# A ConvFFN's up projection as seven sub-products in PSUM, and its down projection in a phase of its own

## The chip, the cores and the metric

The kernel runs on one core of a Trainium2 chip. The metric is device microseconds from start to end of one launch; lower is better. The engines are called as in the profile: PE (matmul), PEld (its weight loads), DVE, ACT, POOL and SP; SP's queue issues all DMAs here.

## The reference, cut to what matters

One layer: a token mixer (a Fourier branch and a gated DeltaNet branch), then a ConvFFN. The change lies in the ConvFFN and in the stage just ahead of it. T = 1024 tokens, D = 1024 channels, D_FF = 2816, all fp32; the tokens form a grid of 16 by 64.

```python
def ffn_sublayer(stream, shift, scale, gate, g_pre, g_post, w_up, conv_w, w_down, rows, cols):
    h = modulate(rms_norm(stream, g_pre), shift, scale)
    a, u = jnp.split(h @ w_up, 2, axis=-1)
    a = dwconv2d(a, conv_w, rows, cols)
    y = (jax.nn.silu(a) * u) @ w_down
    return stream + gate * rms_norm(y, g_post)
```

Here `a` is the gate, which goes through a 3x3 depthwise convolution, and `u` the value. `stream` is the mixer's output, `x + gt1 * rms_norm(merged @ w_out)`.

## The kernel before, in words

**Precision.** Every fp32 factor is split into a high part (rounded to fp32r, a copy) and a low part (the rest, a subtraction). A product of two factors is three matmuls: high by high, high by low, low by high. `halves` loads a weight and splits it (ACT copies the high part, DVE or POOL subtracts), `product` runs the three matmuls per 128 rows of the contraction, `split` splits an activation.

**Order.** The code does not issue instructions where it calls them. It records them (`Program.record`), finds their dependencies through tiles, buffers and banks, and gives each a planned cost; `Program.schedule` then issues them, engine by engine, along their longest paths to the end. Every engine works through its own instructions in that order. All instructions therefore have line 349 in the profile, and tiles are named by number: `p` is a PSUM bank, `m` an SBUF buffer, `d` a buffer in DRAM.

**Ahead of the ConvFFN** (from L1460). For each of eight tiles of 128 tokens, `w_out` is multiplied with the merged branches (48 matmuls of 128x512 into two banks), `post` squares the result on ACT, takes the root on POOL, scales it and adds the residual on DVE. The tile is stored to `x1d`, normed again, and after four tiles (one half of the tokens, g = 0 or 1) transposed on PE: eight transposed blocks per half, which ACT modulates (`hh`), DVE casts to a high part and POOL subtracts to a low part: `h2H[k][g]`, `h2L[k][g]` (L1484 to L1488).

**The ConvFFN** goes over 22 chunks of 128 hidden channels. `up_a(c)` (L1507) multiplies the gate's 1024x128 weights with both halves of the tokens, 24 matmuls of 128x512 for each; ACT copies the result into a padded grid `apad`; DVE runs the nine taps of the convolution over 128x1024 in SBUF (`acc`, one TENSOR_SCALAR and eight SCALAR_TENSOR_TENSOR, L1515 to L1520), ACT takes tanh for the silu, DVE finishes it. `up_u(c)` (L1527) does the value's 48 matmuls, multiplies with `acc` on DVE and splits the gated product into `gH`, `gL`.

After every group of two or three chunks (`groups`, L1538) `down` multiplies these with their rows of `w_down`: for each of the eight token tiles 6 matmuls per chunk into two banks, and DVE adds the banks to `y2[t]`, an fp32 sum in SBUF. In the last group each token tile is squared, scaled by its root and by the gate row, added to `x1d`'s rows, which are loaded into one of two buffers, and stored.

So the up projection has 22 x 2 x 2 x 24 = 2112 matmuls of 128x512 and the down projection 22 x 8 x 6 = 1056. PSUM has eight banks: X0, X1, Y0, Y1, pd, pm, pp, pf; up alternates between pp and pf, down takes the six others.

Of the kernel before, what the change touches and what calls it, by code (L numbers as in the profile page):

```python
# [16 lines left out]
P = 128  # L17
# [470 lines left out]
def layer(prog, a, out):  # L488
# [23 lines left out]
    # ---------------------------------------------------------------- constants  # L512
# [12 lines left out]
    # ---------------------------------------------------------------- weights  # L525
# [33 lines left out]
    # ---------------------------------------------------------------- hidden states  # L559
# [12 lines left out]
    # ---------------------------------------------------------------- modulation, pre-norm  # L572
# [93 lines left out]
    # ---------------------------------------------------------------- decay and beta  # L666
# [75 lines left out]
    # ---------------------------------------------------------------- conv of q, k, v  # L742
# [30 lines left out]
    # ---------------------------------------------------------------- delta rule: preparation  # L773
# [86 lines left out]
    def merge_blocks(name, LTs, bk, k2):  # L860
# [11 lines left out]
        # 32 -> 64  # L872
# [30 lines left out]
        # 64 -> 128  # L903
# [19 lines left out]
    # ---------------------------------------------------------------- context pass  # L923
# [128 lines left out]
    # ---------------------------------------------------------------- latent pass  # L1052
# [185 lines left out]
    # ---------------------------------------------------------------- Fourier branch  # L1238
# [68 lines left out]
    # ---------------------------------------------------------------- branch gates, gated delta output  # L1307
    mp = pool("mH", bufs=17, side="right")
# [90 lines left out]
    mf = [[m_tile(mp, f"mf{k}{g}", F32) for g in range(2)] for k in range(KT)]  # L1399
# [13 lines left out]
    # ---------------------------------------------------------------- merge of the branches  # L1413
    lp = pool("mL", bufs=17, side="right")
# [4 lines left out]
    for k in range(KT):  # L1419
        wl = weights(a["wf"][k], f"wf{k}")  # L1420

        def usef(g, hs, pt):
            t_ = gt.tile([P, HALF], F32, tag="t", name=f"tf{k}{g}")
            gl = gt.tile([P, HALF], F32, tag="gl", name=f"g0l{k}{g}")
            sp.dma_start(gl, gd[0, k, :, hs])
            ve.scalar_tensor_tensor(t_, gl, 1.0, pt, op0=ALU.add, op1=ALU.mult)
            ve.tensor_tensor(t_, t_, mf[k][g], op=ALU.add)
            mH[k][g] = h_ = m_tile(mp, f"mH{k}{g}")
            mL[k][g] = l_ = m_tile(lp, f"mL{k}{g}")
            se.activation(h_, t_, AF.Copy, scale=0.5)  # L1430
            ve.scalar_tensor_tensor(l_, t_, 0.5, h_.bitcast(F32), op0=ALU.mult, op1=ALU.subtract)
# [16 lines left out]
    def post(y2, res, grow_, name, pl, tags=("jk", "pt"), nb=2):  # L1448
        sq = const.tile([P, 2], F32, tag="sq", name=f"sq_{name}", bufs=4)
        for g in range(2):  # L1450
            se.activation(pl.tile([P, HALF], F32, tag=tags[0], name=f"jk_{name}{g}", bufs=nb), y2[g], AF.Square,
                          scale=D ** -0.5, accum_out=sq[:, g:g + 1])
        mean_pow(sq)
        for g in range(2):
            hs = slice(g * HALF, (g + 1) * HALF)
            t_ = pl.tile([P, HALF], F32, tag=tags[1], name=f"pt_{name}{g}", bufs=nb)
            ve.scalar_tensor_tensor(t_, y2[g], sq[:, 1:2], grow_[:, hs], op0=ALU.mult, op1=ALU.mult)
            ve.tensor_tensor(res[:, hs], res[:, hs], t_, op=ALU.add)

    xn = []  # L1460
    for t in range(8):
        xt = wp.tile([P, D], F32, tag="xt", name=f"xr{t}", bufs=6)
        sp.dma_start(xt, a["x"][t * P:(t + 1) * P, :])
        pts = [ps(f"{'XY'[g]}{t % 2}", [P, HALF], f"wo{t}{g}") for g in range(2)]
        n = 0
        for k in range(KT):
            ts_ = slice((t % 4) * P, (t % 4 + 1) * P)
            for m_, w_ in ((mH[k][t // 4], wo[k][0]), (mH[k][t // 4], wo[k][1]), (mL[k][t // 4], wo[k][0])):
                for g in range(2):
                    te.matmul(pts[g], m_[:, ts_], w_[:, g * HALF:(g + 1) * HALF], start=n == 0, stop=n == 23)  # L1470
                n += 1
        post(pts, xt, g1r, f"o{t}", wp)
        sp.dma_start(x1d[t * P:(t + 1) * P, :], xt)
        ss = rms(xt, f"n2_{t}", wp.tile([P, D], F32, tag="junk", name=f"junk2_{t}", bufs=1))
        ve.tensor_scalar(xt, xt, ss, None, op0=ALU.mult)
        xn.append(xt)
        if t % 4 == 3:
            g = t // 4

            def dst(k):  # L1480
                h2H[k][g] = m_tile(mp, f"h2H{k}{g}")
                h2L[k][g] = m_tile(lp, f"h2L{k}{g}")
                return h2H[k][g], h2L[k][g]
            for k in range(KT):  # L1484
                pt = transposed(xn[-4:], k, f"h2{g}", ("pd", "pm")[k % 2])
                hh = wp.tile([P, HALF], F32, tag="hh", name=f"hh{k}{g}")
                se.activation(hh, pt, AF.Identity, scale=mod2[:, 8 + k:9 + k], bias=mod2[:, k:k + 1])
                split(*dst(k), hh, ve, po)  # L1488
# [3 lines left out]
    # ---------------------------------------------------------------- ConvFFN  # L1492
    yp = pool("y2", bufs=1)
    y2 = [yp.tile([P, D], F32, name=f"y2_{t}") for t in range(8)]
    dwp = pool("wd", bufs=3)
    fpl = pool("ffn", bufs=2, side="right")
    cf = fpl.tile([P, NC_FF, 9], F32, name="cf", bufs=1)
# [6 lines left out]
    def h2(g):
        return lambda k: (h2H[k][g], h2L[k][g])

    def up_a(c):  # L1507
        wl = weights(a["wu"][c], f"ua{c}")
        ap_ = apad[c % 2]

        def use(g, hs, pt):
            se.activation(ap_[:, 1 + 8 * g:9 + 8 * g, 1:GW + 1], pt.rearrange("p (a b) -> p a b", b=GW), AF.Copy)
        proj_rows(wl, h2, f"ua{c}", use)
        acc = fpl.tile([P, GR, GW], F32, tag="acc", name=f"acc{c}")
        ve.tensor_scalar(acc, ap_[:, 1:GR + 1, 1:GW + 1], cf[:, c, 4:5], None, op0=ALU.mult)  # L1515
        for i in range(9):
            if i != 4:
                dy, dx = i // 3, i % 3
                ve.scalar_tensor_tensor(acc, ap_[:, dy:dy + GR, dx:dx + GW], cf[:, c, i:i + 1], acc,
                                        op0=ALU.mult, op1=ALU.add)  # L1520
        acc = acc.rearrange("p a b -> p (a b)")
        th_ = fpl.tile([P, T], F32, tag="th", name=f"th{c}", bufs=1)
        se.activation(th_, acc, AF.Tanh)
# [128 lines left out]
```

## Time and profile before

| what | us |
|---|---|
| runs, median of 3 (lowest to highest) | 2151.86 (2146.21 to 2153.07) |
| profiled execution, span from first to last instruction | 2152.6 |
| first ConvFFN weight load issued (trace) | 1263.2 |
| last token tile of `w_out` squared by ACT (trace) | 1373.0 |
| first store of the output issued (trace) | 2114.2 |

The profile comes from one execution of its own, of which the page gives the span alone. Views used below: the page (busy time by engine, and in 40 slices), windows (busy time of each engine in stretches), groups (instructions of one engine, operation and shape: count, busy time, mean ns of one, idle time ahead of them and what ended it), the chain of work that ended last, and the timeline (start, length, engine, operation, count, and in brackets the idle time ahead and its releaser).

### The profile page before, as it was taken

To read this page: it belongs to the slowest core of one execution; us is meant where nothing else is said; L and a number is where in the kernel's file an instruction comes from. 1 tells how busy PE (TensorE), PEld (TensorE's weight loads), DVE (VectorE), ACT (ScalarE), POOL (GpSimd) and SP (SyncE) were. 2 spreads that over 40 slices of the span, in tenths; PEclk is the share of its full clock that TensorE was granted. 3 is DMA by queue.
4 is the path that set the end of the run, shared out by engine and by line. 5 is a ranking of instruction groups with operands and counts; after the bars stand their busy time and mean duration, and the time that the engine had idled before them with its cause. 6 is when DMAs were issued, how large, how long until landed. Compare 5 with 4: busy or idle time off the path is not lost. (4 is left out here: it accounts for less than half of the span.)

```text
span 2152.6 us, 31012 instructions
## 1 busy us (share of the span) xinstructions
PE 2023.2 (94%) x11734; PEld 1623.3 (75%) x11734; DVE 1378.7 (64%) x2608; ACT 740.5 (34%) x1740; POOL 486.8 (23%) x479
## 2 busy tenths in 40 slices
PE   6989999898979989999999999989999999999996
PEld 2777878786768777788777778768888888888885
DVE  7548767676677566653656492587465757475655
ACT  6365454453244433533421142422231222112212
POOL 4131121324233442441311000412010110101005
PEclk9999999899999999999999999989999999999998
DMA  7152323462342444332778561311111111111114
GB/s 274 47 190 83 105 84 126 130 195 66 97 134 84 120 128 114 101 105 76 230 251 292 165 220 42 105 40 44 40 59 35 54 49 45 50 45 50 49 49 147
DMA packets 164216, 232.32 MB, mean 108 GB/s; under 512 B 74097, under 2 KB 87250, under 8 KB 164066
## 3 DMA queue, kind: packets, MB, share of 16 engines
q1 hardware_dynamic: 164066, 230.34, 33.3%
q8 instruction: 92, 1.51, 0.3%
q14 instruction: 58, 0.48, 0.1%
HBM read 180.89 MB, written 49.40 MB: 107 GB/s over the span
## 5 line engine op out<-in xcount | busy, mean ns | idle before, releaser
L349 PE MATMUL p<-m,m 128*128 128x512 f32 (+5 forms) x11574 | 2009.4, 340 | 106.2 <-DVE m L349 65.5
L349 PEld LDWEIGHTS p<-m,m 128*128 128x128 f32 (+3 forms) x11574 | 1604.4, 174 | 501.6 <-ACT m L349 68.8
L349 POOL TENSOR_TENSOR m<-m,m 128x512 fp32r<-128x512 f32 (+6 forms) x244 | 380.5, 1572 | 1332.0 <-ACT m L349 532.6
L349 ACT ACTIVATE m<-m 128x512 fp32r<-128x512 f32 (+6 forms) x563 | 390.3, 711 | 775.0 <-DMA m<-in_wu_dram 254.4
L349 DVE TENSOR_TENSOR m<-m,m 128x512 fp32r<-128x512 f32 (+23 forms) x940 | 483.3, 521 | 192.7 <-ACT m L349 166.4
L349 DVE SCALAR_TENSOR_TENSOR m<-m,m,m 128x1024 f32<-128x1024 f32 (+2 forms) x260 | 304.2, 1176 | 37.8 <-DMA m<-in_w_ada_dram 24.4
L349 ACT ACTIVATE m<-p 128x128 f32<-128x128 f32 (+5 forms) x444 | 181.7, 427 | 336.9 <-PE p L349 309.2
L349 DVE SCALAR_TENSOR_TENSOR m<-p,m,m 128x128 f32<-128x128 f32 (+4 forms) x472 | 191.0, 442 | 110.3 <-ACT m L349 57.6
L349 ACT ACTIVATE m<-p,m 128x128 f32<-128x128 f32 (+2 forms) x240 | 115.6, 492 | 235.8 <-PE p L349 219.8
L349 DVE TENSOR_TENSOR m<-m,p 128x512 f32<-128x512 f32 (+3 forms) x229 | 123.8, 569 | 105.9 <-PE p L349 105.8
L349 DVE SCALAR_TENSOR_TENSOR m<-m,m 128x512 f32<-128x512 f32 (+6 forms) x141 | 107.0, 768 | 36.6 <-ACT m L349 29.1
L349 DVE COPY m<-p 32x256 f32<-32x256 f32 (+10 forms) x116 | 42.0, 367 | 64.0 <-ACT m L349 38.5
L349 POOL COPY m<-m 32x256 f32<-32x256 f32 (+2 forms) x136 | 53.6, 397 | 115.3 <-DMA m<-d 73.5
L349 DVE SCALAR_TENSOR_TENSOR m<-m,m,p 128x128 f32<-128x128 f32 x128 | 42.8, 342 | 41.5 <-PE p L349 40.2
L349 DVE TENSOR_SCALAR m<-m,m 128x1024 f32<-128x1024 f32 x44 | 35.2, 799 | 49.1 <-ACT m L349 36.0
L349 POOL MEMSET m<- 128x1024 f32 (+7 forms) x79 | 35.1, 456 | 134.9 <-PE p L349 101.6
L349 ACT ACTIVATE p<-p 128x128 f32<-128x128 f32 x208 | 55.3, 266 | 20.6 <-PE p L349 18.6
L349 DVE STREAM_TRANSPOSE m<-m 32x256 f32<-32x256 f32 (+1 forms) x50 | 24.5, 491 | 29.1 <-DMA m<-d 28.4
L349 DVE CAST m<-m 128x512 fp32r<-128x512 f32 (+3 forms) x45 | 26.3, 593 | 25.0 <-ACT m L349 23.4
L349 ACT ACTIVATION_READ_ACCUMULATOR p<-p 128x1 f32 x208 | 40.0, 192 | 0.0
L349 DVE TENSOR_TENSOR m<-p,m 128x512 f32<-128x512 f32 (+4 forms) x47 | 28.1, 608 | 11.9 <-PE p L349 11.7
L349 POOL TENSOR_SCALAR_AFFINE_SELECT m<-m 128x1024 f32<-128x1024 f32 x16 | 19.0, 1207 | 72.2 <-DVE m L349 72.2
(20 smaller groups left out, 130.4 us busy)
## 6 DMA issues: line engine op xcount, KB each, us to landing
m<-d SPq DMA_DIRECT2D x76, 512.0 KB
m<-d SPq DMA_DIRECT2D x114, 256.0 KB
m<-in_wi_dram SPq DMA_DIRECT2D x106, 256.0 KB
m<-in_w_ada_dram SPq DMA_DIRECT2D x48, 512.0 KB
d<-m SPq DMA_DIRECT2D x94, 256.0 KB
m<-in_wu_dram SPq DMA_DIRECT2D x88, 256.0 KB
m<-in_wn_dram SPq DMA_DIRECT2D x22, 512.0 KB
m<-in_x_dram SPq DMA_DIRECT2D x16, 512.0 KB
```

Source lines behind the costliest of these rows:

```text
L349: return getattr(engine.real, method)(*[real(v) for v in args], **{k_: real(v) for k_, v in kw.items()})
```

## The change

**The up projection becomes a 2x2 block product.** For each chunk the weights are four 128x512 blocks: gate and value (`a`, `u`), by the lower and upper half of the contraction (`a0`, `a1`, `u0`, `u1`). The hidden state is four blocks too: halves of the contraction by halves of the tokens. Instead of eight block products there are seven, of sums of blocks (Strassen's):

- M2 = (u0+u1) H00, M5 = (a0+a1) H11, M1 = (a0+u1)(H00+H11), M4 = u1 (H10-H00), M3 = a0 (H01-H11), M7 = (a1-u1)(H10+H11), M6 = (u0-a0)(H00+H01).
- Bank A gets M2, then M4 and M7 on top; bank B gets M5, then M3 and M6; bank C gets M1. Between these steps the bank is read: A after M2 by ACT (into `v_`, negated), after M4 by ACT (the value of the first tokens), after M7 by DVE; B after M5 by DVE, after M3 by ACT (the gate of the second tokens), after M6 by DVE. `v_` = M1 - M2 - M5.

Each M is 12 matmuls of 128x512 (`chain`), 84 for a chunk, 1848 in all. The sums of weight blocks (five for a chunk) and all seven low parts of a chunk are formed on POOL, the high parts copied by ACT (`summed`, `split_w`). The sums of the hidden state's blocks are formed once, ahead of the chunks, 16 of them and 28 splits in seven rings of four (`sum_b`, `side_b`), by DVE, POOL and ACT.

**The convolution** runs in two halves of 128x512 whose running sum `acc` lies in a PSUM bank (pd, pm); ACT forms its first tap. The gated product is not split at once but stored to DRAM (`gdr`).

**The down projection is a phase of its own**, after all chunks, in blocks of three, three and two token tiles. Each block keeps its banks over all 22 chunks, so there is no sum in SBUF: 1056 matmuls as before. It loads its part of `gdr`, splits it on ACT and POOL, and keeps 20 of the 22 chunks' split `w_down` rows in SBUF. In the last three chunks of a block the tiles follow one another, and each is normed, added and stored as soon as its bank is complete.

**Ahead of it**, the last two token tiles of `w_out` run side by side (the other six one after another as before), the second norm uses the same helper as the first (`root`), and pools and bank names change.

```diff
-    mp = pool("mH", bufs=17, side="right")
+    mp = [pool(f"mH{g}", bufs=9, side="right") for g in range(2)]
...
-    lp = pool("mL", bufs=17, side="right")
+    lp = [pool(f"mL{g}", bufs=8, side="right") for g in range(2)]
...
+    rings = {1: (mp[0], mp[0]), 3: (lp[0], lp[0]), 4: (mp[1], mp[1]), 2: (lp[1], lp[1])}
+    RB = {}
+    def side_b(m, src, n):
+        hp, lp_ = rings[m]
+        h_, l_ = m_tile(hp, f"bH{m}{n}"), m_tile(lp_, f"bL{m}{n}")
+        (ve.tensor_copy(h_, src) if n % 2 else se.activation(h_, src, AF.Copy))
+        (ve, po)[n % 2].tensor_tensor(l_, src, h_.bitcast(F32), op=ALU.subtract)
+        RB.setdefault(m, []).append((h_, l_))
+    def sum_b(m, x_, y_, op, n):
+        t_ = hb.tile([P, HALF], F32, tag="hs", name=f"hs{m}{n}", bufs=2)
+        (ve, po)[(m + n) % 2].tensor_tensor(t_, x_, y_, op=op)
+        side_b(m, t_, n)
...
-    for t in range(8):
+    for ts in ((0,), (1,), (2,), (3,), (4,), (5,), (6, 7)):
...
+        for k in (0, 4, 1, 5, 2, 6, 3, 7) if g == 0 else (4, 5, 6, 7, 0, 1, 2, 3):
+            pt = transposed(xn[-4:], k, f"h2{g}", ("pd", "pm")[k % 2])
+            hh[k, g] = hb.tile([P, HALF], F32, tag=f"hh{g}", name=f"hh{k}{g}")
+            se.activation(hh[k, g], pt, AF.Identity, scale=mod2[:, 8 + k:9 + k], bias=mod2[:, k:k + 1])
+            if g == 0 and k < 4:
+                side_b(1, hh[k, 0], k)
+            elif g == 0:
+                sum_b(3, hh[k, 0], hh[k - 4, 0], ALU.subtract, k - 4)
+            elif k >= 4:
+                side_b(4, hh[k, 1], k - 4)
+    for i in range(4):
+        sum_b(2, hh[i, 1], hh[i + 4, 1], ALU.subtract, i)
...
+    def chain(pt, w_, m, start):
+        n = 0
+        for i in range(4):
+            ks = slice(i * P, (i + 1) * P)
+            h_, l_ = RB[m][i]
+            for x_, r_ in ((w_[0], h_), (w_[0], l_), (w_[1], h_)):
+                te.matmul(pt, x_[:, ks], r_, start=start and n == 0, stop=n == 11,
+                          skip_group_check=not start)
+                n += 1
+    def split_w(src, name, fresh=None):
+        h_ = wq.tile([P, HALF], F32R, tag="h", name=f"qh_{name}", bufs=WH)
+        se.activation(h_, src, AF.Copy)
+        l_ = wq.tile([P, HALF], F32R, tag="l", name=f"ql_{name}", bufs=WL) if fresh else wq.over(src, F32R, f"ql_{name}")
+        po.tensor_tensor(l_, src, h_.bitcast(F32), op=ALU.subtract)
+        return h_, l_
+    def both(c):
...
+        chain(A, summed("u0", "u1", ALU.add, "m2"), 1, True)
+        se.activation(v_, A, AF.Copy, scale=-1.0)
+        chain(B, summed("a0", "a1", ALU.add, "m5"), 4, True)
+        ve.tensor_tensor(v_, v_, B, op=ALU.subtract)
+        chain(C, summed("a0", "u1", ALU.add, "m1"), 0, True)
+        ve.tensor_tensor(v_, v_, C, op=ALU.add)
+        chain(A, split_w(raw["u1"], f"m4{c}", True), 3, False)
+        se.activation(u_[:, 0:HALF], A, AF.Copy)
+        chain(B, split_w(raw["a0"], f"m3{c}", True), 2, False)
+        se.activation(inner(1), grid(B), AF.Copy)
+        chain(A, summed("a1", "u1", ALU.subtract, "m7"), 6, False)
+        ve.tensor_tensor(inner(0), grid(A), grid(v_), op=ALU.add)
+        chain(B, summed("u0", "a0", ALU.subtract, "m6"), 5, False)
+        ve.tensor_tensor(u_[:, HALF:T], B, v_, op=ALU.add)
+        for g in range(2):
+            hs = slice(g * HALF, (g + 1) * HALF)
+            acc = ps(("pd", "pm")[g], [P, GR // 2, GW], f"acc{c}{g}")
+            se.activation(acc, inner(g), AF.Copy, scale=cf[:, c, 4:5])
...
+            ve.tensor_tensor(th_, th_, u_[:, hs], op=ALU.mult)
+            sp.dma_start(gdr[c, :, hs], th_)
...
+    for blk, ts in enumerate(((0, 1, 2), (3, 4, 5), (6, 7))):
...
+        for n, c in enumerate(first[:-tail]):
+            gs[c] = down_g(c)
+            for t in ts:
+                down_mm(t, c, n)
...
+        for t in ts:
+            for n, c in enumerate(first[-tail:]):
+                down_mm(t, c, NC_FF - tail + n)
+            xt = fin.tile([P, D], F32, tag="xt", name=f"xo{t}")
+            sp.dma_start(xt, x1d[t * P:(t + 1) * P, :])
+            r = root(pts[t], f"f{t}", fin)
```

How the order of the instructions moves shows best where the hidden state's second half is ready and the first chunk begins. **POOL, before:** the end of the hidden state's splits. The eight rows with a size of 128x512 are low parts (a modulated block minus its high part); the last one is the first low part of a gated product, some chunks later.

```order
L349 TENSOR_TENSOR m_10430<-m_10965,m_10416 128x512
L349 TENSOR_TENSOR m_10474<-m_10970,m_10463 128x512
L349 TENSOR_TENSOR m_10479<-m_10965,m_10469 128x512
L349 TENSOR_TENSOR m_10546<-m_10970,m_10530 128x512
L349 TENSOR_TENSOR m_10538<-m_10965,m_10526 128x512
L349 TENSOR_TENSOR m_10598<-m_10970,m_10587 128x512
L349 TENSOR_TENSOR m_10590<-m_10965,m_10580 128x512
L349 TENSOR_TENSOR m_10646<-m_10970,m_10636 128x512
L349 TENSOR_TENSOR m_11460<-m_11349,m_11454 128x512 x2
```

**POOL, now,** the same place, up to the first operation for chunk 1's weights: m_10992 and m_10965 are sums of two blocks of the hidden state (`hs`), the rows that read m_10992 make its low part (those of m_10965 are made on DVE); m_11234 is the low part of u0 - a0 of chunk 0, m_11176 the sum u0 + u1 of chunk 1.

```order
L350 TENSOR_TENSOR m_10992<-m_10928,m_11256 128x512
L350 TENSOR_TENSOR m_11234<-m_11165,m_11209 128x512
L350 TENSOR_TENSOR m_11351<-m_10992,m_11343 128x512
L350 TENSOR_TENSOR m_10992<-m_10989,m_11270 128x512
L350 TENSOR_TENSOR m_11369<-m_10992,m_11365 128x512
L350 TENSOR_TENSOR m_10992<-m_10961,m_11256 128x512
L350 TENSOR_TENSOR m_10965<-m_10923,m_11292 128x512
L350 TENSOR_TENSOR m_11380<-m_10992,m_11378 128x512
L350 TENSOR_TENSOR m_10992<-m_11198,m_11270 128x512
L350 TENSOR_TENSOR m_10965<-m_10984,m_11308 128x512
L350 TENSOR_TENSOR m_11390<-m_10992,m_11388 128x512
L350 TENSOR_TENSOR m_11176<-m_11128,m_11126 128x512
```

Where POOL had eight low parts and then nothing for long, it now has, between the second half's first low part and m_11176 (both counted), 19 operations of this size, two of them for chunk 0's weights and one, the last, for chunk 1's.

**PE, now,** at the same place (pieces in order; p_124 is bank C with M1 of chunk 0, p_192 bank A of chunk 1 with M2, p_197 bank A of chunk 0 with M4):

```order
L350 MATMUL p_124<-m_11365,m_11215 128x512
L350 MATMUL p_124<-m_11369,m_11215 128x512
L350 MATMUL p_124<-m_11365,m_11241 128x512
L350 MATMUL p_192<-m_10933,m_11215 128x512
L350 MATMUL p_192<-m_10271,m_11215 128x512
L350 MATMUL p_197<-m_10286,m_11114 128x512
L350 MATMUL p_197<-m_10339,m_11114 128x512
L350 MATMUL p_197<-m_10286,m_11187 128x512
```

Two products of chunk 1, which need the copy of m_11176, stand ahead of M4 of chunk 0; M2, M5 and M1 of chunk 0, 36 products, stand ahead of them and behind the last product of `w_out`. Before, 142 products of the up projection stood between the last product of `w_out` and the first product of chunk 2's gate.

More of the change, by code (lines that the diff above doesn't have):

```diff
@@ L1489, in layer @@
     close(wp)
     close(wop)
[L1493 to L1497, printed above, removed]
+    wq = pool("wq", bufs=5, side="right")
+    wq.sizes = {"r": HALF}
+    RAW, WH, WL = 8, 5, 5
+    h2p = pool("h2p", bufs=24, side="right")
+    for m in (0, 6, 5):
+        rings[m] = (h2p, h2p)
+    for i in range(4):
+        sum_b(2, hh[i, 1], hh[i + 4, 1], ALU.subtract, i)
@@ L1498, in layer @@
+    for i in range(4):
+        sum_b(0, hh[i, 0], hh[i + 4, 1], ALU.add, i)
+    for i in range(4):
+        sum_b(6, hh[i + 4, 0], hh[i + 4, 1], ALU.add, i)
+    for i in range(4):
+        sum_b(5, hh[i, 0], hh[i, 1], ALU.add, i)
+    close(hb)
+    upr = pool("upr", bufs=1, side="right")
+    gst = pool("gst", bufs=4)
+    upl = pool("upl", bufs=1)
+    cf = upl.tile([P, NC_FF, 9], F32, name="cf")
     sp.dma_start(cf, a["cf"])
     ve.tensor_scalar(cf, cf, 0.5, None, op0=ALU.mult)
-    apad = [fpl.tile([P, GR + 2, GW + 2], F32, name=f"apad{i}", bufs=1) for i in range(2)]
+    apad = [upl.tile([P, GR + 2, GW + 2], F32, name=f"apad{i}") for i in range(2)]
@@ L1501, in layer @@
     for t_ in apad:
         po.memset(t_, 0.0)
[L1504 to L1508, printed above, removed]
-        ap_ = apad[c % 2]
[L1511 to L1523, printed above, removed]
-        ve.scalar_tensor_tensor(acc, th_, 1.0, acc, op0=ALU.add, op1=ALU.mult)
-        return acc
@@ L1527, in up_u @@
-    def up_u(c, acc):
-        wl = weights(a["wu"][NC_FF + c], f"uu{c}")
-        gH = fpl.tile([P, T], F32R, tag="gH", name=f"gH{c}", bufs=4)
-        gL = fpl.tile([P, T], F32R, tag="gL", name=f"gL{c}", bufs=4)
-        def use(g, hs, pt):
-            ve.tensor_tensor(acc[:, hs], acc[:, hs], pt, op=ALU.mult)
-            split(gH[:, hs], gL[:, hs], acc[:, hs], se, po)
-        proj_rows(wl, h2, f"uu{c}", use)
-        return gH, gL
-    groups = [3, 3, 3, 3, 3, 2, 2, 3]
-    g2r = yp.tile([P, D], F32, name="g2r")
@@ L1540, in layer @@
[L1540 to L1556 removed]
+    gdr = dram.tile([NC_FF, P, T], F32, name="gdr")
@@ new lines, in layer, with down_w @@
+    for c in range(NC_FF):
+        both(c)
+    for p_ in (upr, h2p, wq, lp[1], lp[0], mp[1], mp[0], upl):
+        close(p_)
+    wn = pool("wn", bufs=1, side="right")
+    fin = pool("fin", bufs=2)
+    g2r = fin.tile([P, D], F32, name="g2r", bufs=1)
+    sp.dma_start(g2r, grow[1:2, :].broadcast_to([P, D]))
+    held = {}
+    def down_w(c, at):
+        if held.get(at, (None,))[0] != c:
+            h_ = wn.tile([P, D], F32R, tag=f"h{at}", name=f"dh{c}_{at}")
+            w_ = wn.tile([P, D], F32, tag=f"l{at}", name=f"dw{c}_{at}")
+            sp.dma_start(w_, a["wn"][c * P:(c + 1) * P, :])
+            held[at] = (c, (h_, split_over(wn, h_, w_, f"dl{c}_{at}")))
+        return held[at][1]
@@ L1566, in down @@
[L1566 to L1584 removed]
+                t_ = fin.tile([P, HALF], F32, tag="pt", name=f"pf{t}{g}")
```

171 lines of the change are left out of this document (98 added, 73 removed).

## The prediction

> **What bounds the kernel now.** I read the page first, then windows over the ConvFFN, then the chain of waits, then the groups and the timeline at the two ends of the ConvFFN.
>
> ```profile
> PE 2023.2 (94%) x11734; PEld 1623.3 (75%) x11734; DVE 1378.7 (64%) x2608; ACT 740.5 (34%) x1740; POOL 486.8 (23%) x479
> ...
> 1600.00:1800.00 200.00, 200.00 (x861) 160.87 (x860) 125.51 (x132) 40.30 (x59) 18.75 (x13) 1.00 0.14 47
> 1800.00:2000.00 200.00, 200.00 (x864) 161.44 (x863) 127.32 (x133) 42.26 (x62) 20.00 (x13) 1.00 0.15 48
> ...
> 1655.63 100.66 PE p L349 x432
> 1756.30 100.43 PE p L349 x432
> ```
>
> The page says PE, 94%. The windows (length; then busy time and instructions of PE, PEld, DVE, ACT, POOL; granted clock, DMA share, GB/s) say it for the ConvFFN alone: PE is busy for all of 200 us at full clock, POOL for a tenth, DMA for 15%. The chain of waits has nothing but PE there: 432 products, which is three chunks of up and down, in 100.43 us, **0.2325 us a product** (864 in 200 us gives the same). In this stage a product less is 0.2325 us less, as long as no other engine becomes later than PE.
>
> At the two ends of the ConvFFN PE does wait:
>
> ```profile
> 1373.02 0.60 ACT L349 ACTIVATE m<-p 128x512 f32<-128x512 f32 x1 [3.33 <-PE p L349]
> 1375.33 1.40 DVE L349 SCALAR_TENSOR_TENSOR m<-p,m,m 128x512 f32<-128x512 f32 x2
> 1375.49 1.29 POOL L349 TENSOR_TENSOR m<-m,m 128x512 fp32r<-128x512 f32 x1 [0.39 <-DVE m L349]
> 1376.65 1.29 DVE L349 TENSOR_TENSOR m<-m,m 128x512 f32<-128x512 f32 x2
> 1386.00 1.28 POOL L349 TENSOR_TENSOR m<-m,m 128x512 fp32r<-128x512 f32 x1 [5.03 <-DVE m L349]
> 1389.30 1.28 POOL L349 TENSOR_TENSOR m<-m,m 128x512 fp32r<-128x512 f32 x1 [0.36 <-DVE m L349]
> 1389.78 1.08 DVE L349 CAST m<-m 128x512 fp32r<-128x512 f32 x1 [0.56 <-ACT m L349]
> 1390.94 1.27 POOL L349 TENSOR_TENSOR m<-m,m 128x512 fp32r<-128x512 f32 x1 [0.36 <-DVE m L349]
> 1427.14 3.32 PE L349 MATMUL p<-m,m 128*128 128x512 f32 x7 [4.94 <-DVE m L349]
> ...
> 2079.67 52.51 PE L349 MATMUL p<-m,m 128*128 128x512 f32 x227
> 2147.62 1.42 DVE L349 SCALAR_TENSOR_TENSOR m<-m,m,m 128x512 f32<-128x512 f32 x2 [1.22 <-DMA m<-d]
> ```
>
> At the **hand-over** from `w_out` to the ConvFFN, ACT squares the last token tile at 1373.02, so its products have just ended. 13.0 us later (1386.00) POOL makes the first low part of the hidden state's second half. Up to 1427.14, 54.1 us, PE runs the 142 products that stand there in its order, worth 33.0 us: **21.1 us are lost**. At the **end** the last product is over at 2079.67 + 52.51 = 2132.2 and the span ends at 2152.6: a tail of **20.4 us**, in which output tiles are loaded, added and stored through two buffers.
>
> **The change, part by part.** The sum is made against the profiled span, 2152.6, which is 0.7 above the median of the runs.
>
> *Products removed.* A chunk's up projection falls from 96 products to 84, over 22 chunks 264 products: 264 x 0.2325 = **61.4 us less**, if PE stays the bound. The down projection's 1056 products keep their number, shape and order of banks; I take the same rate. PE's time for a chunk is 84 x 0.2325 = 19.5 us, and each other engine must fit into that.
>
> ```profile
> L349 DVE SCALAR_TENSOR_TENSOR m<-m,m,m 128x1024 f32<-128x1024 f32 x96 | 123.2, 1284 | 2.4
> ...
> L349 DVE TENSOR_TENSOR m<-m,p 128x512 f32<-128x512 f32 x156 | 100.3, 684 | 75.2 <-PE p L349 75.1
> L349 DVE TENSOR_TENSOR m<-m,m 128x512 f32<-128x512 f32 x48 | 32.1, 697 | 9.8 <-DMA m<-d 9.8
> L349 DVE SCALAR_TENSOR_TENSOR m<-m,m,m 128x512 f32<-128x512 f32 x32 | 31.4, 1011 | 9.1 <-DMA m<-d 5.8 <-POOL m L349 3.0
> L349 DVE SCALAR_TENSOR_TENSOR m<-m,p 128x512 f32<-128x512 f32 x32 | 21.3, 683 | 11.0 <-PE p L349 6.6 <-DMA m<-d 4.1
> L349 DVE SCALAR_TENSOR_TENSOR m<-p,m,m 128x512 f32<-128x512 f32 x16 | 11.3, 746 | 4.0 <-POOL m L349 4.0
> ...
> L349 ACT ACTIVATE m<-m 128x512 fp32r<-128x512 f32 x294 | 181.9, 629 | 544.2 <-DMA m<-in_wu_dram 254.4 <-PE p L349 117.5 <-DVE m L349 81.6
> L349 ACT ACTIVATE m<-p,m 128x512 f32<-128x512 f32 x80 | 56.8, 721 | 124.9 <-PE p L349 110.6 <-POOL m L349 9.7 <-DVE m L349 4.5
> L349 ACT ACTIVATE p<-m 128x512 f32<-128x512 f32 x16 | 9.4, 588 | 24.6 <-DVE m L349 24.6
> ...
> 1501.25 3.91 POOL L349 TENSOR_TENSOR m<-m,m 128x512 fp32r<-128x512 f32 x2 [20.30 <-ACT m L349]
> ```
>
> *POOL* gets 12 operations a chunk (five sums, seven low parts) where it had two. Alone one takes 1.28 (1386.00). Beside DVE work it takes longer: 3.91 for two at 1501.25. The rows at 1389 show how: a DVE cast begins while POOL works, ends only 0.36 after POOL's operation, and then POOL goes on, so two such operations exclude each other. At 1375.33 two DVE operations that read one tensor from PSUM and one from SBUF run beside POOL's, and neither is longer than alone (1.40 for two, 1.29). The new DVE work of a chunk is nearly all of that kind: the convolution's sum, four evictions and two silu steps each have their second tensor in PSUM. Only two multiplications by `u_` read two tensors from SBUF, 0.70 each. So 12 x 1.28 + 2 x 0.70 = 16.8 us, under 19.5. The bounds are 15.4 (nothing in the way) and 12 x 1.96 = 23.5 (all as at 1501.25); I take 16.8, as the rows at 1375 are the nearer.
>
> *DVE* writes into PSUM, which no row of before shows. Its 16 taps of 128x512: the nearest rows are the 746 ns of an operation that reads PSUM and a scalar, and two of these in 1.40, that is 0.66 from start to start; in the order the two halves' taps mostly alternate, so that one seldom waits for the one just ahead. ACT's rows show no price for a PSUM target (588 against 629). From below 16 x 0.66 = 10.6, from above 16 x 1.01 = 16.2 (the group with three SBUF operands); I take 0.70, 11.2. Four evictions at 0.684, two silu steps at 0.683 and two multiplications at 0.697 make 5.5 more. 16.7 us, under 19.5; the ends are 16.1 and 21.7.
>
> [...]
>
> *ACT*: seven copies (0.63), three evictions and two first taps (0.72 at most), two tanh (0.63): 9.3 us, hidden. *DMA*: four 256 KB loads as before and two 256 KB stores, 1.5 MB in 19.5 us, about 80 GB/s; in the down phase 0.7 MB in 18 x 0.2325 = 4.2 us, 170 GB/s. The window below moved 236 GB/s while PE worked for 99% of it, so I cost the way through DRAM at nothing. Were that cover gone, each 10% of the down phase would cost 1056 x 0.2325 x 0.1 = 25 us.
>
> ```profile
> 1000.00:1200.00 200.00, 198.24 (x873) 153.37 (x872) 118.52 (x169) 56.43 (x110) 39.26 (x29) 1.00 0.71 236
> ```
>
> *Sums in SBUF removed.* 112 DVE additions (684 ns) and 16 ACT copies of the old down projection go. They lay beside PE, which never waited there: nothing gained. *Up to down:* the split rows of `w_down` lie over the rings of the hidden state, and the first ring ends with M2 of the last chunk, six sub-products (72 products, 16.7 us) before the end; load, copy and subtraction fit. What is late next is the first tile in banks X1 and Y1, which must wait until DVE has evicted the last chunk: 0.25 + 0.68 + 0.25, with the same at block ends, **1.5 us**, bounds 0 and 8.
>
> *The hand-over* gets worse. Count from T, the square of the last token tile. T + 13.0 as before until the first low part. Then POOL has 19 operations up to the sum for chunk 1's weights: 24.3 us at 1.28. Beside them DVE has 15 sums and low parts with two SBUF inputs (0.70) and eight casts (0.36), 13.4 us, and these and POOL's exclude each other. So that sum is ready between T + 37.3 and T + 50.7; both queues are dense, so I take T + 48, near the upper end. ACT copies it (0.63) and PE goes on at T + 48.7. The products of chunk 0 that follow (M4, M3, M7, M6) and everything after are queued behind the waiting one, though M4's operands have long been there; ahead of it PE had 36 products, 8.4 us. Lost: 40.3 instead of 21.1, **19.2 us more**, bounds 8.5 and 22. The slow products after such a wait (7 in 3.32 us at 1427.14) come in both. After it POOL, at 16.8 us a chunk, gains on PE.
>
> *The tail* gets shorter. All token tiles but the last are stored under PE, and the last one's rows of `x1d` are already loaded. The steps are those at 1373.02: from the square to the end of the second addition (1376.65 + 1.29) 4.9 us, 0.25 ahead of it, and from the last DVE operation (2147.62 + 1.42 = 2149.0) to the end of the span 3.6: 8.8 us instead of 20.4, **11.6 us less**, bounds 8 and 12.
>
> Sum: 2152.6 - 61.4 + 1.5 + 19.2 - 11.6 = 2100.3, against the median 0.7 less: **2100 us**, 2.4% faster.
>
> **The rivals.**
>
> 1. *The cheap hand-over* (0.15): DVE's work there falls into POOL's gaps. T + 37.3 holds, 10.7 us less: 2089. For it: POOL waited 0.36 between operations at 1389, so there are gaps; against it: that wait was DVE's own use of the lock.
> 2. *PE waits in each chunk* (0.22): its order runs three sub-products side by side, and bank B's next sub-product needs DVE's subtraction from `v_`, behind taps already begun. One tap (0.70) and a release (0.3) late in each chunk is 22 x 1.0: 2122. For it: DVE would be busy for 86% of a chunk. Against it: M1 and M4 stand between, up to 24 products, 5.6 us.
> 3. *DVE paces the up phase* (0.06): above (19.5 - 5.5)/16 = 0.875 us a tap DVE is later than PE. At 0.95 it is 20.7 us a chunk, 1.2 x 22 = 26 more: 2126.
> 4. *POOL paces it, and the kernel is slower* (0.07): this begins where a POOL operation takes 19.5/12 = 1.63 on average. It eats all the gain (51.6 us, 2.35 a chunk) at 1.82. At the 1.96 of 1501.25 a chunk takes 23.5, 4.0 x 22 = 88 more: 2188. For it: before shows just this price wherever POOL worked in the ConvFFN beside taps. Against it: those taps had three operands in SBUF, the new ones have their sum in PSUM.
>
> That products don't go is no rival: the order has 264 fewer.
>
> **How the numbers follow.** My forecast has 0.47, for 2095 to 2110; the rivals 0.15, 0.22, 0.06 and 0.07; 0.03 is left for a total between, within 0.3% of before, which is about what a measurement of this kernel can tell from no change. The range goes from 2084 (cheap hand-over with an up-to-down step of nothing and the tail's best) to 2128 (rivals 2 and 3); it leaves out rival 4 and the rest, and some of each edge. Faster by over 0.3%: 0.90, within 0.3%: 0.03, slower: 0.07.
>
> **What would show it.** In the changed profile, 84 products a chunk at 0.23 us without idle time; POOL near 1.3 us an operation in the up phase and 80 to 90% busy, DVE near 85%; a PE wait of 10 us or more on ACT or POOL before chunk 1's first product; about 9 us from the last product to the end. The prediction fails if chunks take over 20.5 us, if POOL's mean is over 1.6, or if the down phase waits for DMA.

## The result, and the profile after

The changed kernel takes **2098.5 us** (median of 4 runs, 2097.32 to 2099.22) against 2151.24 of the kernel before beside it (4 runs): the ratio is 0.9754, 95% interval 0.9742 to 0.9765, 2.5% faster. The forecast was 2100. Its profiled span is 2096.8 us, 55.8 less than before's.

First the page of after (busy time, share of the span and instructions of each engine), then two windows, one in the up phase and one in the down phase (start and end; length; busy time and instructions of PE, PEld, DVE, ACT, POOL; granted clock, DMA share, GB/s):

```profile
PE 1960.3 (93%) x11470; PEld 1580.9 (75%) x11470; DVE 1355.2 (65%) x2714; ACT 827.6 (39%) x1934; POOL 822.5 (39%) x757
...
1450.00:1830.00 380.00, 379.29 (x1674) 313.64 (x1673) 333.17 (x469) 168.94 (x285) 319.72 (x243) 1.00 0.26 90
1850.00:2070.00 220.00, 220.00 (x937) 176.47 (x936) 57.99 (x72) 47.43 (x96) 63.50 (x64) 1.00 0.32 103
```

264 products are gone (11734 - 11470), and PE is the bound of both phases: it waits 0.7 us in the 380 of the first window and not at all in the second. But a product takes 380/1674 = 0.227 us in the up phase and 220/937 = 0.235 us in the down phase, where the prediction had 0.2325 for both. POOL is busy for 84%, DVE for 88%.

The groups of DVE and POOL between 1500 and 1800 us (busy time, mean ns of one; idle time before them):

```profile
L350 DVE SCALAR_TENSOR_TENSOR p<-m,m,p 128x512 f32<-128x512 f32 x252 | 171.4, 749 | 2.2
L350 DVE TENSOR_TENSOR m<-m,m 128x512 f32<-128x512 f32 x32 | 40.9, 1301 | 0.5
...
L350 POOL TENSOR_TENSOR m<-m,m 128x512 fp32r<-128x512 f32 x110 | 149.1, 1365 | 29.0 <-PE p L350 23.8 <-ACT m L350 5.1
L350 POOL TENSOR_TENSOR m<-m,m 128x512 f32<-128x512 f32 x80 | 106.3, 1329 | 19.4 <-PE p L350 19.3 <-POOL m L350 0.2
```

The taps, whose sum is in PSUM, take 749 ns, and POOL's operations 1.33 to 1.37 us beside them. The multiplications by `u_`, with two tensors from SBUF, take 1.30 us where 0.70 was priced; they are the only DVE operations here with both tensors in SBUF.

The hand-over, from the timeline (start, length, engine, operation; idle time before it and who ended it):

```profile
1372.41 0.58 ACT L350 ACTIVATE m<-p 128x512 f32<-128x512 f32 x1
...
1419.02 2.76 POOL L350 TENSOR_TENSOR m<-m,m 128x512 fp32r<-128x512 f32 x2 [0.36 <-DVE m L350]
1421.82 0.63 ACT L350 ACTIVATE m<-m 128x512 fp32r<-128x512 f32 x1 [2.50 <-POOL m L350]
1422.50 1.22 PE L350 MATMUL p<-m,m 128*128 128x512 f32 x2 [9.81 <-ACT m L350]
1424.30 1.73 DVE L350 TENSOR_TENSOR m<-m,m 128x512 f32<-128x512 f32 x1 [1.20 <-POOL m L350]
1426.12 0.60 ACT L350 ACTIVATE m<-p 128x512 f32<-128x512 f32 x1 [3.68 <-DVE m L350]
1426.77 5.57 PE L350 MATMUL p<-m,m 128*128 128x512 f32 x14 [3.05 <-ACT m L350]
```

T, the square of the last token tile, is at 1372.41. PE goes on at 1422.50 = T + 50.1, as ACT has copied the sum of chunk 1's weights (forecast T + 48.7). Two products later it stops **again**: ACT's next eviction (1426.12, bank A of chunk 0 into `v_`) has waited 3.68 us for a DVE sum that ends at 1426.03 (1424.30 + 1.73). PE has nothing to do with that sum. The prediction had no such wait.

The end (last products; last DVE step):

```profile
2079.71 9.32 PE L350 MATMUL p<-m,m 128*128 128x512 f32 x39
...
2092.33 1.28 DVE L350 TENSOR_TENSOR m<-m,m 128x512 f32<-128x512 f32 x2
```

The last product is over at 2089.03, the span at 2096.8: a tail of 7.8 us instead of 20.4.

### The profile page after: what moved, and what is told of

Read it like the earlier page. It is cut to its first block, busy times and chain, and to the rows that moved or that the text cites. A ratio compares the mean times of both kernels' runs of the same rounds, so it can differ in the third digit from the quotient of the medians.

```text
span 2096.8 us, 31434 instructions
## 1 busy us (share of the span) xinstructions
PE 1960.3 (93%) x11470; PEld 1580.9 (75%) x11470; DVE 1355.2 (65%) x2714; ACT 827.6 (39%) x1934; POOL 822.5 (39%) x757
## 5 line engine op out<-in xcount | busy, mean ns | idle before, releaser
L350 PE MATMUL p<-m,m 128*128 128x512 f32 (+6 forms) x11310 | 1946.5, 339 | 125.9 <-DVE m L350 66.6
L350 PEld LDWEIGHTS p<-m,m 128*128 128x128 f32 (+4 forms) x11310 | 1562.0, 174 | 500.6 <-ACT m L350 78.1
L350 POOL TENSOR_TENSOR m<-m,m 128x512 fp32r<-128x512 f32 (+8 forms) x522 | 716.8, 1393 | 946.9 <-ACT m L350 424.2
L350 ACT ACTIVATE m<-m 128x512 fp32r<-128x512 f32 (+8 forms) x655 | 428.0, 668 | 651.9 <-DMA m<-d 165.7
L350 DVE TENSOR_TENSOR m<-m,m 128x512 f32<-128x512 f32 (+23 forms) x940 | 512.0, 552 | 74.5 <-ACT m L350 53.0
L350 ACT ACTIVATE m<-p 128x512 f32<-128x512 f32 (+4 forms) x510 | 220.0, 447 | 329.9 <-PE p L350 290.4
L350 DVE SCALAR_TENSOR_TENSOR p<-m,m,p 128x512 f32<-128x512 f32 x352 | 240.1, 748 | 3.0
L350 DVE SCALAR_TENSOR_TENSOR m<-m,m 128x512 f32<-128x512 f32 (+5 forms) x119 | 76.4, 649 | 27.7 <-ACT m L350 19.6
L350 DVE TENSOR_TENSOR m<-m,p 128x128 f32<-128x128 f32 (+3 forms) x117 | 53.4, 458 | 33.2 <-PE p L350 32.4
L350 DVE SCALAR_TENSOR_TENSOR m<-m,m,m 128x1024 f32<-128x1024 f32 (+2 forms) x68 | 59.6, 877 | 23.6 <-DMA m<-in_w_ada_dram 23.2
```

The source lines that it names most:

```text
L350: return getattr(engine.real, method)(*[real(v) for v in args], **{k_: real(v) for k_, v in kw.items()})
```

## The experiments

Medians are of each kernel's own runs. A ratio is to the kernel before on the same chip, with its 95% interval; for the changed kernel it is 0.9754.

### Moving addresses only

What differs between the two phases is not the instruction. The stationary tiles of the down products, `gh` and `gl`, lie on the left stack of SBUF behind the constants, whose size (1603 words) is odd; those of the up products lie on the right stack, at whole multiples of 64 bytes (all such places are counted by the pools' sizes, from the start of the kernel's SBUF area in a partition). Three kernels differ from the changed one in unused words alone; all instructions keep their order on every engine.

```
     held = {}
+    const.tile([P, 13], F32, name="pad")     # 1 and 5 words in the other two
```

> The changed kernel with 13 words of unused space behind the constants: same instructions, same order, but every tile of the left stack starts 52 bytes further on (the stationary tiles gh and gl of the down products at a multiple of 64 bytes in a partition, and not 12 bytes behind one). Theory 'placement' (a product whose stationary tile starts off such a boundary goes slower): the down products go from one every 0.2353 us to one every 0.2267 us, as the up products do, so 1056 x 0.0086 = -9.1 us there, a few us more from the mixer's products whose tiles stand 12 bytes off, together 2084 to 2090 us against 2098.5. Rival 'stage' (the rate belongs to the pattern of the down products, two products of one stationary tile into two banks): step stays 0.235, time 2097 to 2100.

> The same with 1 word of unused space: the left stack starts at 16 bytes behind a multiple of 64, on a multiple of 16 but not of 32. Theory 'placement' with a 16-byte boundary: as with 13 words, down products at 0.2267 us, 2084 to 2090 us. 'Placement' with a boundary of 32 or 64 bytes: little or nothing gained, down products still above 0.230 us, 2094 to 2100. Rival 'stage': 0.235, 2097 to 2100.

> The changed kernel with 5 unused words behind the constants: the stationary tiles of the down products start 32 bytes behind a multiple of 64 (12 behind one in the changed kernel: 0.2353 us a product; 16 behind: 0.2319; at one: 0.2268). If the boundary that counts is 32 bytes, 0.2268 us and 2086 to 2090; if it is 64 bytes, about 0.229 to 0.234 us and 2090 to 2098.

The down window of the three (13 words, 1 word, 5 words):

```profile
1850.00:2070.00 220.00, 220.00 (x972) 182.10 (x971) 56.26 (x70) 47.32 (x97) 64.63 (x67) 1.00 0.33 104
```

```profile
1850.00:2070.00 220.00, 220.00 (x951) 178.02 (x950) 55.36 (x69) 45.54 (x94) 63.93 (x66) 1.00 0.32 101
```

```profile
1850.00:2070.00 220.00, 220.00 (x944) 176.72 (x943) 57.84 (x72) 47.23 (x96) 63.49 (x64) 1.00 0.33 104
```

| unused words | offset of `gh`, `gl` mod 64 bytes | products in 220 us | time | ratio |
|---|---|---|---|---|
| 0 | 12 | 937 | 2098.5 | 0.9754 |
| 1 | 16 | 951 | 2097.43 | 0.9740 (0.9724 to 0.9755) |
| 5 | 32 | 944 | 2097.19 | 0.9755 (0.9724 to 0.9787) |
| 13 | 0 | 972 | 2087.12 | 0.9696 (0.9682 to 0.9711) |

PE has no idle time in any of these windows, at full clock. Of the four places only the multiple of 64 bytes makes the down products as fast as the up products; 16 and 32 are not enough. 1056 products gain 8.9 us by it (1056 x (0.2348 - 0.2263)), the kernel 11.4 (its profiled span 9.5). The rest was not followed up; T alone, ahead of all this, moves by up to 3.45 us between these four kernels, from 1368.96 with 1 word to 1372.41 with none. "Stage" is refuted for these products.

The same for the kernel before, and then with the moving tile of its down products at a wider boundary (432 more words behind the tiles `y2`, ahead of the pool `dwp`):

```
+    const.tile([P, 13], F32, name="pad")
     ...
+    fpl.tile([P, 2], F32, name="pad2")
     cf = fpl.tile([P, NC_FF, 9], F32, name="cf", bufs=1)
```

> The kernel before with the same 13 words, and 2 words more ahead of cf on the right stack, so that the stationary and the moving tiles of the up products and of the down products all start at a multiple of 64 bytes. 'Placement': up products from 0.2336 to about 0.227 us (2112 x 0.0066 = -14), down products from 0.230 to 0.227 (1056 x 0.0035 = -3.7), a few us more in the mixer: 2130 to 2136 us, and of the change's gain some 8 us was placement. Rival 'stage': 2149 to 2153.

> The kernel before as in the run with 13 words, with 432 more unused words, so that the moving tile of its down products starts at a multiple of 2048 bytes instead of 320 bytes behind one, as all moving tiles do that went at 0.2267 us. Theory 'the moving tile needs a wider boundary': its down products go from 0.2305 to 0.227 us, 1056 x 0.0035 = -3.7 us, 2136 to 2140 us. Rival 'interleaving' (the down products of this kernel are slower since they alternate with up products or share banks with the sums): 0.2305 stays, 2141 to 2144.

One window over the ConvFFN, of before, of before with 13 + 2 words, and with 432 more:

```profile
1450.00:2070.00 620.00, 620.00 (x2669) 499.47 (x2668) 396.26 (x408) 137.85 (x204) 62.45 (x38) 1.00 0.14 47
```

```profile
1450.00:2070.00 620.00, 619.92 (x2702) 504.95 (x2701) 397.34 (x411) 137.03 (x202) 61.32 (x38) 1.00 0.15 47
```

```profile
1450.00:2070.00 620.00, 619.61 (x2695) 503.42 (x2694) 393.73 (x410) 136.30 (x201) 58.45 (x36) 1.00 0.15 47
```

2142.34 us (ratio 0.9956, 0.9939 to 0.9972) and 2139.84 (0.9937, 0.9922 to 0.9952). The 13 + 2 words make before 0.4% faster, less than the expected 2130 to 2136: the 33 products more in 620 us (7.5 us) come from the up products, which go from 0.2333 to 0.2291 us from the start of one to that of its neighbour (0.2273 in the changed kernel), while the down products stayed at 0.230. The 432 words don't change that. That run's time lies inside the theory's 2136 to 2140 all the same, but it is no evidence for it, as the down products were to gain and didn't. Its interval meets that of the run with 13 + 2 words, and so many unused words make the planner's order another one from the hand-over on. Nor does the edit do what its expectation says: the moving tiles that went at 0.2267 lie 1856 bytes behind a multiple of 2048, not at one. Why before's down products are slower even at multiples of 64 bytes is open; that they run mixed with up products was not tested by itself.

### The second stop at the hand-over

By the pools' sizes `v_` of chunk 0 takes words 10704 to 11215 of SBUF, and `hh31`, a modulated block of the hidden state, takes 10307 to 10818 until the ring sums are done. The last ring sum, `hs53`, reads `hh31`. So the eviction of M2 must wait for the last of the ring sums, because of 115 shared words. The experiment takes `v_` from its pool ahead of `u_`:

```
+        v_ = upr.tile([P, HALF], F32, tag="v", name=f"v{c}", bufs=2)
         u_ = upr.tile([P, T], F32, tag="u", name=f"u{c}", bufs=3)
-        v_ = upr.tile([P, HALF], F32, tag="v", name=f"v{c}", bufs=2)
```

> The changed kernel with the tile v_ taken from its pool ahead of u_: v_ of chunk 0 then lies where no tile of the ring sums lay (in the changed kernel its last words fell on hh31, which the last ring sum hs53 reads), so the eviction of bank A after M2 no longer waits for hs53. Theory 'overlap': the second stall at the hand-over, 3.05 us of PE behind ACT's eviction, goes or falls below 1 us; the hand-over from the last product of the projection to the steady products shortens by 2 to 3.5 us and the time is 2095 to 2097. Rival 'sums': PE only waits for the last ring sums at a later product instead (M6's weights and sums come last), the hand-over and the time stay within 1 us of 2098.5.

PE's timeline in it:

```profile
1397.68 3.36 PE L350 MATMUL p<-m,m 128*128 128x512 f32 x14
1401.63 4.73 PE L350 MATMUL p<-m,m 128*128 128x512 f32 x19 [0.60 <-ACT m L350]
```

2086.44 us (ratio 0.9691, 0.9668 to 0.9714), outside the expected 2095 to 2097: 12 us gained, four times the expected. The right theory, but the wait that the trace named was only its end. Since the planner sees that bank A of chunk 0 isn't free for long, it puts M4 and all behind it after M2 of chunk 1. With the 115 words gone, M4 and M3 run right behind M5, at 1399 to 1406, and the wait of 9.81 at 1422.50 goes with the one of 3.05: no wait of PE behind them is over 1.82 us.

The 62 us from T on, of the changed kernel and of this one:

```profile
1372.00:1434.00 62.00, 29.71 (x93) 19.43 (x94) 41.85 (x43) 21.06 (x37) 47.89 (x38) 0.64 0.10 36
```

```profile
1375.00:1437.00 62.00, 42.14 (x144) 28.27 (x145) 45.97 (x46) 24.22 (x44) 53.84 (x42) 0.75 0.10 34
```

Of the PE instructions 32 are transposes in both. So 61 products against 112: 51 more, worth 51 x 0.227 = 11.6 us.

### Both edits, and what is left of the hand-over

> The changed kernel with both edits of the first round: v_ taken ahead of u_, and 13 unused words behind the constants. If the two gains are of different causes they add: down products at 0.2267 us (-9.1 us) and a hand-over that loses 37.7 us of PE instead of 49.8 (-12.1), 2075 to 2080 us. Rival: they have one cause (the moved addresses alone), and the time stays near 2086.

2077.06 us (ratio 0.9651, 0.9633 to 0.9670): they add. Two more steps from there. `v_` gets a pool of its own on words that are free at T:

```
     wq.sizes = {"r": HALF}
     RAW, WH, WL = 8, 5, 5
+    vp = pool("vp", bufs=2, side="right")
     h2p = pool("h2p", bufs=24, side="right")
...
-        v_ = upr.tile([P, HALF], F32, tag="v", name=f"v{c}", bufs=2)
+        v_ = vp.tile([P, HALF], F32, tag="v", name=f"v{c}")
```

> The combined kernel, but with v_ in a pool of its own ahead of the ring tiles, where the words are free as soon as the projection's last product is done (in the combined kernel v_ of chunk 0 falls on the buffer of xr4, which the transposes of the second token half still read). Theory 'overlap': the 12 products of M4 of chunk 0 move into the 14 us in which PE waits between M2 and M5, the hand-over shortens by about 12 x 0.2268 = 2.7 us, 2073 to 2076 us against 2077. Rival 'sums': the end of the hand-over is set by VectorE's and POOL's ring sums, M4 only runs earlier and PE waits as much more later: 2076 to 2080.

2076.72 us (0.9642, 0.9614 to 0.9669). M4 does move ahead of M5, but the time doesn't tell the theory from its rival: the interval is wider than the effect. Nor do the 62 us from T on: 145 PE instructions here, 132 in the combined kernel, but 144 in the kernel with the moved `v_` alone, whose order of instructions is the combined kernel's. Then, in addition, POOL leaves the token blocks to DVE and ACT:

```
 def side_b(m, src, n):
-    (ve.tensor_copy(h_, src) if n % 2 else se.activation(h_, src, AF.Copy))
-    (ve, po)[n % 2].tensor_tensor(l_, src, h_.bitcast(F32), op=ALU.subtract)
+    se.activation(h_, src, AF.Copy)
+    ve.tensor_tensor(l_, src, h_.bitcast(F32), op=ALU.subtract)
 def sum_b(m, x_, y_, op, n):
-    (ve, po)[(m + n) % 2].tensor_tensor(t_, x_, y_, op=op)
+    ve.tensor_tensor(t_, x_, y_, op=op)
```

> The same with all sums and low halves of the token blocks on VectorE and all their copies on ScalarE, POOL left with the weights' sums alone during the hand-over. Theory 'exclusion' (in the hand-over VectorE and POOL wait for one another, 1.3 us for an instruction that takes 0.72 us alone): 24 fewer POOL instructions at 1.3 us for 24 more of VectorE at 0.7 us, the hand-over shortens by 3 to 8 us: 2066 to 2073 us. Rival 'queue' (VectorE's queue is what sets the hand-over, and gets longer): same or slower, 2075 to 2085.

The 62 us from T on, of the kernel with `vp` and of this one:

```profile
1369.00:1431.00 62.00, 43.49 (x145) 29.69 (x146) 45.71 (x43) 22.66 (x41) 54.06 (x40) 0.78 0.10 33
```

```profile
1366.00:1428.00 62.00, 45.54 (x172) 31.55 (x171) 50.91 (x60) 34.17 (x62) 38.49 (x29) 0.89 0.14 49
```

**2069.68 us** (0.9619, 0.9599 to 0.9639), the fastest of all and inside the expected 2066 to 2073, with 27 products more in these 62 us (6.1 us). By time alone the step isn't clear, as its interval meets that of the kernel with `vp`; the windows speak for it, with more than twice the 12 by which the two kernels of one order differ. They don't show that the exclusion is the cause: the edit also moves the 14 casts of these splits from DVE to ACT, and it moves 24 operations (10 of the 20 sums, of which the description of the change counts 16, and 14 of the 28 low parts) from an engine that needs 1.28 us for one to an engine priced at 0.70. That the two engines hold each other up there is rather to be seen in DVE's groups of the changed kernel, from T to T + 62, where 0.70, 0.70 and 0.36 us were priced:

```profile
L350 DVE TENSOR_TENSOR m<-m,m 128x512 f32<-128x512 f32 x11 | 15.8, 1441 | 2.0 <-POOL m L350 1.2 <-ACT m L350 0.5
L350 DVE TENSOR_TENSOR m<-m,m 128x512 fp32r<-128x512 f32 x11 | 11.5, 1044 | 5.0 <-ACT m L350 5.0
L350 DVE CAST m<-m 128x512 fp32r<-128x512 f32 x11 | 8.6, 781 | 4.9 <-ACT m L350 2.5 <-POOL m L350 2.3
```

### The scheme by itself

Eight block products a chunk, no sums of weights and none of token blocks, all else as in the changed kernel:

```
+        w = {k: split_w(raw[k], f"{k}{c}", True) for k in ("a0", "a1", "u0", "u1")}
+        for pt, k, ms in ((A, "a", (1, 3)), (B, "a", (2, 4)), (C, "u", (1, 3)), (E, "u", (2, 4))):
+            chain(pt, w[k + "0"], ms[0], True)
+            chain(pt, w[k + "1"], ms[1], False)
+        se.activation(inner(0), grid(A), AF.Copy)
...
-        chain(A, summed("u0", "u1", ALU.add, "m2"), 1, True)
...
```

> The changed kernel with the plain eight block products a chunk (96 products instead of 84) and so without sums of weights and without sums of token blocks: rings hold the four blocks of the projected tokens alone; the two phases, the DRAM round trip, the convolution in PSUM and the down phase stay. Theory 'PE-bound scheme' (what the seven products save is their PE time, what they cost is the ring sums at the hand-over): the up phase gets 264 x 0.2268 = 59.9 us more of products, the hand-over loses 20 to 30 us instead of 49.8, POOL falls to about 5 us of work a chunk: 2125 to 2140 us. Rival 'sums' (the sums cost about as much as the products saved): 2100 or less. By the prediction's own terms this kernel stands at before plus 1.5 less 11.6, with a hand-over as before's: some 2140.

From T on and in the up phase:

```profile
1372.00:1434.00 62.00, 59.47 (x267) 46.44 (x267) 47.10 (x63) 31.71 (x54) 27.08 (x23) 1.00 0.37 125
...
1500.00:1800.00 300.00, 296.77 (x1285) 239.07 (x1285) 179.83 (x267) 93.32 (x164) 69.62 (x54) 1.00 0.22 72
```

2129.11 us (0.9888, 0.9872 to 0.9905), 30.6 slower than the changed kernel. By T + 62 it has 174 products more (39.5 us); it has 264 more to do (59.9 us); and in its up phase a product takes 300/1285 = 0.2335 us, 7 ns more than in the changed kernel (300/1325), over the 1877 that are left at T + 62 that is 13 us. These 7 ns are waits and not slower products: in both kernels the median product starts 0.227 us behind its neighbour, but here 40 in the 300 us start 0.3 us or more behind it, 8.1 us in all, of which the profile shows 3.2 as PE waiting for ACT. 59.9 + 13 - 39.5 = 33, near the 30.6 measured: of the time that seven products save on PE, two thirds go back at this hand-over. In the fastest kernel, with the sums on DVE, it is a third: 95 products (267 against 172), 21.6 us.

The prediction's terms put this kernel at some 2140. It is 11 us faster, and the hand-over has room for that: 61 PE instructions more than before in the same 62 us (267 against 206), 14 us. So the new order without sums has a better hand-over than before's, where the terms took them as equal.

### The convolution's sum in SBUF

```
-            acc = ps(("pd", "pm")[g], [P, GR // 2, GW], f"acc{c}{g}")
+            acc = upl.tile([P, GR // 2, GW], F32, tag="acc", name=f"acc{c}{g}", bufs=2)
```

> The changed kernel with the running sum of the nine taps in SBUF instead of PSUM (two tiles, for which the down phase has three buffers of the gated product instead of four). Theory 'shared port' (rival 4 of the prediction: a VectorE instruction with all operands in SBUF and POOL's exclude one another): POOL's 14 instructions a chunk go from 1.35 to about 1.9 us or wait as long, POOL needs 25 us or more a chunk and paces the up phase: chunk period above 23 us, time above 2180 us. Rival 'no port': POOL stays at 1.35, the period at 19.04 and the time within 10 us of 2098.

Windows and groups between 1500 and 1800 us:

```profile
1500.00:1800.00 300.00, 237.80 (x921) 186.51 (x920) 282.47 (x262) 92.56 (x155) 215.21 (x133) 0.90 0.17 57
...
L350 DVE SCALAR_TENSOR_TENSOR m<-m,m,m 128x512 f32<-128x512 f32 x174 | 216.3, 1302 | 2.0 <-DVE m L350 0.5
...
L350 POOL TENSOR_TENSOR m<-m,m 128x512 fp32r<-128x512 f32 x77 | 127.8, 1668 | 42.0 <-ACT m L350 29.6 <-PE p L350 12.4
```

2271.82 us (1.0551, 1.0529 to 1.0572). Where the sum lies decides, and both sides get slower: a tap goes from 749 to 1302 ns, POOL's operation (12 a chunk, not 14) from 1365 to 1668. Before's taps, all in SBUF but with POOL idle for most of the time, took 1284 ns for twice the size. What paces is DVE (94% busy), not POOL (72%): 921 products in 300 us are 27 us a chunk.

### The tail

```
-        tail = 3
+        tail = 1
```

> The changed kernel with one held-back chunk instead of three in each group of token tiles: tile 6's last product comes 6 products ahead of tile 7's (1.4 us) instead of 18 (4.2 us). Theory 'order' (the short tail comes from tile 6's epilogue lying under tile 7's products): the end of the span lies 2 to 3 us further behind the last product, 10 to 11 us instead of 8.1, time 2100 to 2102. Rival 'buffers' (the short tail is one tile's epilogue whatever the order): tail 8.1 to 8.6, time within 1 us of 2098.5.

The last products of this kernel:

```profile
2077.63 8.63 PE L350 MATMUL p<-m,m 128*128 128x512 f32 x36
...
2089.94 1.28 DVE L350 TENSOR_TENSOR m<-m,m 128x512 f32<-128x512 f32 x2
```

2094.56 us (0.9737, 0.9713 to 0.9761), a span of 2094.4 and so a tail of 2094.4 - 2086.26 = 8.1 us, 0.3 more. The theory "order" is refuted: tile 7's epilogue is a chain of steps that wait for one another, and tile 6's fits into its gaps. The time is 4 us below what either theory had, and its interval meets the changed kernel's. In the profiled executions the span is 2.4 us shorter, while T lies 3.4 us earlier, at 1369.02, although up to there both kernels issue the same instructions in the same order.

## Why the prediction was right

The direction, the bound and the size came out; the size partly since two errors cancelled. Against before's span, by the prediction's terms:

| term | forecast | measured | from |
|---|---|---|---|
| 264 products | -61.4 | -61.4 | 84 a chunk, at before's 0.2325 |
| rate of the other products | 0 | -7.6 | up 1810 x (0.227 - 0.2325) = -10.0, down 1056 x (0.2348 - 0.2325) = +2.4 |
| hand-over | +19.2 | +24.6 | 1426.77 - 1372.41 less 38 x 0.227: 45.7 lost, not 21.1 |
| tail | -11.6 | -12.6 | 7.8 against 20.4 |
| up to down, rest of PE's small waits | +1.5 | +1.8 | what is left over |
| ahead of T | 0 | -0.6 | 1372.41 against 1373.02 |
| sum | -52.3 | -55.8 | |

- **PE as the bound, POOL and DVE under it**: right. POOL at 16.8 us a chunk was forecast, 84% of 19.0 are 16.0; DVE 16.7, measured 16.7, though with luck in the parts: from 1500 to 1800 us the two multiplications took 1.2 us a chunk more than their price, while the taps took 0.3 less and 0.6 of the groups' busy time overlaps. Rivals 2 to 4 didn't happen: no wait of 1 us a chunk in the up window, taps at 0.749 and not above 0.875, POOL at 1.37 and not above 1.63. The run with the sum in SBUF shows that the condition of rival 4, which operand lies in PSUM, was what mattered: there the kernel is slower than before, though by DVE's taps and not by POOL. A tap took 1302 ns with the sum in SBUF and 749 with it in PSUM; what in the chip makes the difference is not shown.
- **The same rate for all products**: this step failed. The rate of before was taken as that of a product; it was the mean of up products at 0.2333, whose stationary tile lay 12 bytes behind a multiple of 64, and down products at 0.230, whose lay 8 behind one. The change moved the up projection's weights to the right stack, onto multiples of 64 bytes, and the gated product to the left, 12 behind one. The runs with unused words show what that costs the changed kernel's down products, 8.9 us. Before's up products gained 4.2 ns by it (0.2333 to 0.2291), two thirds of their way to the changed kernel's 0.2273; the last 1.8 ns are not shown. So the 7.6 us are in the main a matter of where tiles lie; that nothing of them belongs to the seven products or the separate phases is not shown, as before's down products didn't react to their places.
- **The hand-over**: mechanism right, size 5.4 us too small, beyond the upper bound of 22. "M4's operands have long been there" is the wrong sentence: its operands were, its bank wasn't, since the eviction of M2 waited for `hs53` through 115 words. Rival 1, the cheap hand-over, is refuted for this kernel: T + 50.1, not T + 37.3, and close to the T + 50.7 at which the two engines' work never overlaps. With DVE's operations there at 1.04 and 1.44 us where 0.70 was priced, the exclusion is the likely reason; the run with the sums on DVE doesn't isolate it. (The prediction's row at 1389 is read a little wrong: the cast ends 0.28 after POOL's operation, POOL goes on 0.36 after it. No term rests on that.)
- **Up to down**: PE's only wait between 1450 us and the last product is 0.71 us behind POOL at 1829.40, still in the up phase. The first down product follows the last up product without a stop, so the 1.5 us forecast for bank X1 and Y1 didn't come; the 1.8 in the table is what the other rows leave over.
- **The tail**: the size is right, and so is the chain of the last tile's steps that sets it. "All token tiles but the last are stored under PE" is not: four stores, tile 6's two among them, are issued from 2089.70 on, behind the last product. They cost nothing, since tile 7's steps end later, and the order of the last chunks counts for 0.3 us.

## What to carry to other kernels

Before an order of instructions is blamed for a wait, compare the addresses of the tiles on both sides of it: a few words shared by two phases can chain the first instruction of one to the last of the other, and a planner then builds its order around that. When a rate per product is taken from a profile, take it for each placement of the operands, and try pools padded so that matmul tiles start at multiples of 64 bytes: a few unused words made these two kernels 0.4 to 0.6% faster. A scheme that saves products pays with sums at the start, where nothing hides them, so price that stretch by itself.

## What the runs showed of the hardware that was not expected

- A down product of the changed kernel took 0.226 us with its stationary tile at a multiple of 64 bytes of the kernel's SBUF area, and 0.231 to 0.235 us at 16, 32 or 12 bytes behind one (972 against 951, 944 and 937 in 220 us), with PE busy throughout at full clock. Before's down products took 0.230 us at 8 bytes behind one and at a multiple alike.
- PE's granted clock fell in the waits of the hand-over: 0.64 over the 62 us from T in the changed kernel, 1.00 with eight products. Around the two products at 1422.50, which took 1.22 us, it was 0.50, and from 1428 to 1432, with PE busy throughout, still 0.59: twelve products in 4.0 us, which at 0.227 are 2.7. So these waits cost more than their length.
- DVE's taps and POOL's operations beside them both took longer with the taps' sum in SBUF (1302 and 1668 ns) than with it in PSUM (749 and 1365).
